# A sixth pair of up chunks by seven products in each MLP of a two-layer trunk, with down chunks cut in halves and read in another order

## The chip, the cores and the metric

The kernel runs on one core of a Trainium2 chip. The metric is the device time of one execution in microseconds, as the median of several. TensorE (PE) multiplies matrices into PSUM, its weight loads (PEld) overlap its matmuls; VectorE (DVE) and ScalarE (ACT) do elementwise work; GpSimd (POOL) does little here but issue transfers of its own queue; SyncE (SP) issues all others.

## The reference, cut to what matters

Two layers, each a token mixer and an MLP, all adding into one residual stream of 256 tokens by 2048 columns in float32. The change touches the two MLPs alone:

```python
D_MODEL = 2048; SEQ = 256; DEPTH = 2; D_FF = 4 * D_MODEL

def sq_relu_mlp(h, w_up, w_down):
    a = jax.nn.relu(h @ w_up)
    return (a * a) @ w_down

def reference(...):
    for i in range(DEPTH):
        ...
        h = rms_norm(x, mlp_norm_g[i])
        x = x + sq_relu_mlp(h, mlp_w_up[i], mlp_w_down[i]).astype(x.dtype)
    return x
```

## The kernel before, in words

**Split products.** Every float32 product is made of three: an operand is split into a rounded high part and the rest, and high by high, high by low and low by high are added up in PSUM (L447 to L449 for ordinary products, L1140 to L1142 for the wide ones). The tokens are the stationary side, in two tiles of 128; the weights stream through in tiles of 512 columns.

**Weight stream.** `plan` lists the loads of 256 rows by 512 columns (512 KB, five buffers `raw`), `units` the tiles that are split from them, both in the order in which TensorE will use them. `split` (L398, L399) casts a tile on ScalarE (`wh`) and subtracts on VectorE (`wl`), into five buffers each; it is called once for each unit used, so the splits run up to five units ahead. An ordinary unit is two blocks of 128 rows of one chunk of 512 columns: 2 x 2 token tiles x 3 = 12 matmuls.

**The MLP.** The 8192 inner columns are done in four quarters `b`. Each quarter has four up chunks `n` of 512 columns, each 16 row blocks `k` or 8 units, which give the turned activations `aT[n]`, and then four down chunks, again 16 row blocks each: `k // 4` says which `aT` is read. Up and down of the first quarter are counted from unit 0.

**Wide pairs.** For the pairs in `WIDE` two up chunks are computed together from quarters of the blocks, as a two-by-two product by seven products instead of eight. For each pair of row blocks `pr` there are three tiles (`crossed`, `differences`, `sums`) with two products of three matmuls each, and for each two of them one more tile: 28 tiles of 6 matmuls in all. VectorE makes the difference tile (L395) and the two halves of the sum tile (L401, L402) besides the three splits. `token_sums` makes the same sums of the tokens once per MLP. `WIDE_AT` is written by hand: it says after which ordinary unit each group of wide tiles stands. `wide_chain` then combines six PSUM banks (L1104 to L1111), and `turn_up` squares, transposes (L1058), writes to DRAM by POOL (L1052), loads back by SP (L354) and splits the turned activations (L1083 to L1090). The `free` keys hold the last step back until the previous quarter's `aT` has been read.

**Banks.** While wide work is woven in, six of the eight PSUM banks are its own, and all ordinary products share the two of one tag (`turn["only"]`), one for each token tile. The next product can start in a bank only when ScalarE has emptied it. The down products of the first three quarters are added by `add_chain` with `late`: ScalarE scales them into four small `y` tiles (L995), and POOL issues an accumulating transfer of each into `x` (L996). The last quarter has no wide work beside it at its end: three of its chunks run as a group, in the row parts of `LAST_DOWN_PARTS`, in three pairs of banks, and VectorE adds them (L999). `last_product` does the last chunk.

**Order.** `Jobs` runs the chains as generators: `tick` advances them after each row block or wide tile, so a chain's instructions stand in the engines' queues at the place where it was resumed; `pin` fixes that order on every engine.

Of the kernel before, what the change touches and what calls it, by code (L numbers as in the profile page):

```python
# [12 lines left out]
AF = mybir.ActivationFunctionType  # L13
# [4 lines left out]
P = 128  # L18
D = 2048
S = 256  # L20
# [21 lines left out]
LAST_DOWN_PARTS = ((0, 8), (8, 12), (12, 16))  # L42
# [6 lines left out]
WIDE = ((1, 0), (2, 0), (2, 2), (3, 0), (3, 2))  # L49
WIDE_AT = ((15, 19, 23, 27, 31, 34, 37, 39, 41, 42, 42, 43), (45, 47, 50, 53, 55, 58, 61, 63, 66, 67, 67, 68),  # L50
           (71, 74, 77, 79, 82, 85, 87, 90, 93, 93, 94, 95), (98, 101, 103, 106, 109, 111, 114, 117, 119, 119, 120, 120),
           (122, 125, 127, 130, 133, 135, 138, 141, 143, 143, 144, 145))
UP_ALONE = ((2, 3), (2, 3), (), ())


def wide_slots():

    for (b, n), at in zip(WIDE, WIDE_AT):
# [4 lines left out]
        for pr in range(0, KC // 2, 2):  # L63
            yield at[KC // 2 + pr // 2], (b, n, 3, pr)

# [54 lines left out]
def trunk(ctx: ExitStack, tc, x, fox_w_in, fox_b_f, fox_q_gain, fox_k_gain, fox_w_out, dil_w_in,  # L120
# [56 lines left out]
    wake(*[NC] * 8, S)  # L177
# [103 lines left out]
    def add(w, rows, cols):  # L281

        for r in range(rows[0], rows[1], RAW_SUB * P):
            units.append((len(plan), "rows"))
# [22 lines left out]
    def add_group(*chunks, parts=PARTS):  # L307

        for a, b in parts:
            for w, cols in chunks:  # L310
                add(w, (a * P, b * P), cols)
# [11 lines left out]
    def add_mlp(l):  # L323
# [3 lines left out]
        for b in range(4):  # L327
# [6 lines left out]
            add_group(*((down, [(n * NC, NC)]) for n in range(together)), parts=LAST_DOWN_PARTS)  # L334
            for n in range(together, NX):
                add(down, (0, D), [(n * NC, NC)])
# [100 lines left out]
    def product_steps(acc, keys, lhs, steps, post=None):  # L437

        for k in steps:
            jobs.need(keys(k))  # L440
            i = k % W_SUB
            hi, lo = (in_turn(w[:, i, :]) for w in splits[used[0]])
            ah, al = lhs(k)
            for t in range(NT):
                tok = slice(t * P, (t + 1) * P)
                first, last = k == 0, k == KC - 1
                nc.tensor.matmul(acc[t], ah[:, tok], hi, start=first, stop=False)  # L447
                nc.tensor.matmul(acc[t], ah[:, tok], lo, start=False, stop=False)  # L448
                nc.tensor.matmul(acc[t], al[:, tok], hi, start=False, stop=last)  # L449
            if post is not None and k == KC - 1:  # L450
                jobs.spawn(post(acc))
            if i == W_SUB - 1:
                used[0] += 1
# [868 lines left out]
```

## Time and profile before

| | |
|---|---|
| median of 3 runs | 2083.45 us (2082.98 to 2085.27) |
| span of the profiled execution | 2081.4 us |
| TensorE busy, matmuls | 2076.2 us, 9838 |
| VectorE busy | 1714.8 us |
| ScalarE busy | 1306.1 us |
| GpSimd busy | 275.1 us |
| moved by DMA | 539.04 MB, mean 259 GB/s |

The span is what lies between the first and the last instruction of the profiled execution; the timed runs also hold what lies around it. Busy time is the union of an engine's instructions. Matmuls overlap one another, so their durations don't add up to their time: the step from start to start does that. An engine that works through a queue in order can be idle because it is ahead; whether that matters is read from who waits for it.

### The profile page before, as it was taken

How to read it: one execution, taken by the hardware profiler on the slowest of the kernel's cores; microseconds unless marked ns; L12 is line 12 of the kernel's file. 1: busy time of each engine (PE TensorE's matmuls, PEld its weight loads, DVE VectorE, ACT ScalarE, POOL GpSimd, SP SyncE). 2: the span in 40 equal slices, each digit the busy share in tenths (PEclk: the TensorE clock that was granted, in tenths of full speed). 3: DMA queues.
4: the chain of work that ended last, by engine and by line, in shares of the span. 5: the costliest groups of instructions: out<-in, count | busy, mean ns of one | idle time of the engine just before them, and what ended most of it. 6: DMA issues, size and time to landing. Idle time of an engine off the chain costs nothing.

```text
span 2081.4 us, 28973 instructions
## 1 busy us (share of the span) xinstructions
PE 2076.2 (100%) x9838; PEld 1819.9 (87%) x9838; DVE 1714.8 (82%) x2183; ACT 1306.1 (63%) x1825; POOL 275.1 (13%) x398
## 2 busy tenths in 40 slices
PE   9999999999999999999999999999999999999999
PEld 7888888888888888888888888888888888888888
DVE  6888876898989889888668787766998898899874
ACT  6665654866666667664656565556766676666662
POOL 2000000111212112120010010000113031212120
PEclk9999999999999999999999999999999999999999
DMA  8888887888988898897877876867888888898885
GB/s 258 257 259 261 262 249 213 268 284 265 270 282 265 263 299 272 264 286 246 281 242 230 250 238 211 262 212 236 269 275 264 279 274 266 276 288 277 263 277 168
DMA packets 357205, 539.04 MB, mean 259 GB/s; under 512 B 43752, under 2 KB 144448, under 8 KB 357056
## 3 DMA queue, kind: packets, MB, share of 16 engines
q1 hardware_dynamic: 334624, 507.41, 76.6%
q0 software_dynamic: 22016, 29.38, 6.2%
q8 instruction: 77, 1.26, 0.2%
q10 hardware_dynamic: 416, 0.39, 0.1%
q14 instruction: 72, 0.59, 0.1%
HBM read 484.09 MB, written 40.39 MB: 252 GB/s over the span
## 4 chain that ended last, share of the span: by engine, by line
PE 98%; DVE 1%; ACT 1%; DMA 1%; issue 0%; SPq 0%; ACTq 0%
PE acc L447 26%; PE acc L448 26%; PE acc L449 26%; PE wide_n_tp L1140 2%; PE wide_n_tp L1141 2%; PE wide_n_tp L1142 2%; PE wide_n_sc L1141 2%; PE wide_n_acc L1140 2%; PE wide_n_sc L1140 2%; PE wide_n_acc L1142 2%; PE wide_n_sc L1142 2%; PE wide_n_acc L1141 2%; PE sc_d L800 0%; DVE wl L399 0%; DMA turned_n<-blocks_n 0%; PE sc_f L800 0%
## 5 line engine op out<-in xcount | busy, mean ns | idle before, releaser
L399 DVE TENSOR_TENSOR wl<-raw,wh 128x1024 fp32r<-128x1024 f32 (+1 forms) x763 | 919.9, 1215 | 302.4 <-ACT wh L398 295.2
L398 ACT CAST wh<-raw 128x1024 fp32r<-128x1024 f32 (+1 forms) x763 | 787.3, 1046 | 498.9 <-PE acc L449 370.1
L447 PE MATMUL acc<-wh,hT_n 128*128 128x512 f32 x1280 | 486.3, 380 | 0.0
L448 PE MATMUL acc<-wl,hT_n 128*128 128x512 f32 x1280 | 485.3, 379 | 0.2 <-DVE wl L399 0.2
L449 PE MATMUL acc<-wh,hT_n 128*128 128x512 f32 x1280 | 485.2, 379 | 0.0
L449 PEld LDWEIGHTS acc<-wh,hT_n 128*128 128x128 f32 x1280 | 241.9, 189 | 34.4 <-DVE hT_n L631 0.2
L448 PEld LDWEIGHTS acc<-wl,hT_n 128*128 128x128 f32 x1280 | 242.1, 189 | 33.7 <-DVE wl L399 0.9
L447 PEld LDWEIGHTS acc<-wh,hT_n 128*128 128x128 f32 x1280 | 242.1, 189 | 33.0 <-ACT hT_n L630 0.2
L447 PE MATMUL acc<-wh,aTh_n1a 128*128 128x512 f32 x512 | 194.0, 379 | 0.0
L448 PE MATMUL acc<-wl,aTh_n1a 128*128 128x512 f32 x512 | 194.0, 379 | 0.0
L449 PE MATMUL acc<-wh,aTl_n1a 128*128 128x512 f32 x512 | 194.0, 379 | 0.0
L447 PE MATMUL acc<-wh,aTh_n3a 128*128 128x512 f32 x480 | 181.9, 379 | 0.0
L448 PE MATMUL acc<-wl,aTh_n3a 128*128 128x512 f32 x480 | 181.9, 379 | 0.0
L449 PE MATMUL acc<-wh,aTl_n3a 128*128 128x512 f32 x480 | 181.9, 379 | 0.0
L996 POOL DMA_DIRECT2D x<-y_n x96 | 84.7, 1325 | 480.0 <-ACT y_n L995 421.1
L398 ACT CAST wh<-sd 128x1024 fp32r<-128x1024 f32 x80 | 84.1, 1051 | 101.9 <-DVE sd L395 78.5
L398 ACT CAST wh<-v 128x1024 fp32r<-128x1024 f32 x80 | 84.1, 1052 | 53.8 <-PE acc L449 41.4
L448 PEld LDWEIGHTS acc<-wl,aTh_n1a 128*128 128x128 f32 x512 | 96.8, 189 | 13.8
L449 PEld LDWEIGHTS acc<-wh,aTl_n1a 128*128 128x128 f32 x512 | 96.8, 189 | 13.7
L447 PEld LDWEIGHTS acc<-wh,aTh_n1a 128*128 128x128 f32 x512 | 96.8, 189 | 13.7
L399 DVE TENSOR_TENSOR wl<-v,wh 128x1024 fp32r<-128x1024 f32 x80 | 97.5, 1218 | 5.8 <-ACT wh L398 4.5
L395 DVE TENSOR_TENSOR sd<-raw,raw 128x1024 f32<-128x1024 f32 x80 | 97.4, 1218 | 5.5 <-DMA raw<-in_mlp_w_up_dram 5.5
(665 smaller groups left out, 3216.8 us busy)
## 6 DMA issues: line engine op xcount, KB each, us to landing
raw<-in_mlp_w_up_dram SPq DMA_DIRECT2D x296, 512.0 KB, 4.9
raw<-in_mlp_w_down_dram SPq DMA_DIRECT2D x256, 512.0 KB, 5.1
raw<-in_dil_w_in_dram SPq DMA_DIRECT2D x192, 256.0 KB, 3.5
raw<-in_fox_w_in_dram SPq DMA_DIRECT2D x94, 512.0 KB, 5.0
raw<-in_fox_w_out_dram SPq DMA_DIRECT2D x32, 512.0 KB, 4.9
raw<-in_dil_w_in_dram SPq DMA_DIRECT2D x32, 512.0 KB, 5.4
raw<-in_dil_w_out_dram SPq DMA_DIRECT2D x32, 512.0 KB, 4.5
x<-y_n POOLq DMA_DIRECT2D x96, 128.0 KB, 6.2
```

Of the source, the lines that this page charges most:

```text
L395: nc.vector.tensor_sub(quarters[0], raw, raws[n - 1][:, 1, :].unsqueeze(1).to_broadcast([P, RAW_SUB, NC]))
L398: nc.scalar.copy(hi[:, part, :], raw[:, part, :])
L399: nc.vector.tensor_sub(lo[:, part, :], raw[:, part, :], hi[:, part, :].bitcast(F32))
L447: nc.tensor.matmul(acc[t], ah[:, tok], hi, start=first, stop=False)
L448: nc.tensor.matmul(acc[t], ah[:, tok], lo, start=False, stop=False)
L449: nc.tensor.matmul(acc[t], al[:, tok], hi, start=False, stop=last)
L996: nc.gpsimd.dma_start(xt[n][:, t, h * HC:h * HC + HC], y, accum_op=ALU.add)
L1140: nc.tensor.matmul(banks[bank], ah, wh, start=what < 3 and of == 0, stop=False, **alone)
L1141: nc.tensor.matmul(banks[bank], ah, wl, start=False, stop=False, **alone)
L1142: nc.tensor.matmul(banks[bank], al, wh, start=False, stop=of == KC // 2 - 1, **alone)
```

## The change

It does five things, in both MLPs:

- `WIDE` takes in the pair (1, 2), so chunks 2 and 3 of quarter 1 leave `UP_ALONE`; `WIDE_AT` is written anew for six pairs over the fewer ordinary units, 160 instead of 176 per MLP.
- `HALVED`: in quarters 2 and 3, the first three down chunks are done in two halves of their rows. The first halves come first, each as a product of its own that is added late; the second halves follow, in quarter 3 as the group, whose parts now begin at row block 8.
- `place`: from quarter 1 on, the rows of down are read in the order of `aT[1]`, `aT[0]`, `aT[3]`, `aT[2]`, and the chains of a wide pair wait for `free` and `room` in that order.
- In products that share the one pair of banks, the first and the last unit run both row blocks for one token tile and then for the other, and the chains that empty the banks take the first tile while the second is still being multiplied (`ended`).
- The activations of a wide pair are spread: Relu at once, Square a step later (`turn`), and the evacuated tile's Relu isn't repeated.

The one wake matmul of 256 columns at the start becomes two of 128.

```diff
-LAST_DOWN_PARTS = ((0, 8), (8, 12), (12, 16))
+LAST_DOWN_PARTS = ((8, 12), (12, 16))
-WIDE = ((1, 0), (2, 0), (2, 2), (3, 0), (3, 2))
-WIDE_AT = ((15, 19, 23, 27, 31, 34, 37, 39, 41, 42, 42, 43), (45, 47, 50, 53, 55, 58, 61, 63, 66, 67, 67, 68),
-           (71, 74, 77, 79, 82, 85, 87, 90, 93, 93, 94, 95), (98, 101, 103, 106, 109, 111, 114, 117, 119, 119, 120, 120),
-           (122, 125, 127, 130, 133, 135, 138, 141, 143, 143, 144, 145))
-UP_ALONE = ((2, 3), (2, 3), (), ())
+WIDE = ((1, 0), (1, 2), (2, 0), (2, 2), (3, 0), (3, 2))
+WIDE_AT = ((15, 19, 23, 27, 30, 32, 33, 34, 37, 38, 39, 39),
+           (42, 44, 47, 49, 51, 52, 55, 56, 58, 58, 60, 61),
+           (64, 65, 67, 69, 71, 73, 75, 77, 79, 79, 79, 79),
+           (83, 85, 87, 88, 90, 91, 95, 97, 99, 99, 100, 101),
+           (102, 103, 104, 107, 108, 110, 112, 113, 115, 115, 116, 117),
+           (118, 120, 122, 123, 125, 126, 127, 128, 131, 131, 132, 132))
+UP_ALONE = ((2, 3), (), (), ())
+HALVED = (0, 0, 3, 3)
+HALF = KC // 2
+def place(b, k):
+    return k ^ 4 if b else k
...
-    wake(*[NC] * 8, S)
+    wake(*[NC] * 8, P, P)
...
+            for n in range(HALVED[b]):
+                add(down, (0, D // 2), [(n * NC, NC)], b)
...
+        def three(k, t):
...
+            first, last = k == begin, k == end
...
+        for k in steps[::W_SUB]:
+            rows = range(k, k + W_SUB)
+            by_block = post is not None and (k == begin or k + W_SUB > end)
+            ended = ("ended", used[0])
+            for i in range(W_SUB):
+                for r in rows if by_block and not i else () if by_block else rows[i:i + 1]:
+                    jobs.need(keys(r))
+                for r, t in [(r, i) for r in rows] if by_block else [(rows[i], t) for t in range(NT)]:
+                    three(r, t)
+                if by_block and k + W_SUB > end:
+                    if i:
+                        jobs.reach(ended)
+                    else:
+                        jobs.spawn(post(acc, ended))
...
+        for n in range(halved):
+            product(keys(0), lhs, lambda acc, ended, n=n: add_chain(acc, n, None, None, scale, True, ended), range(HALF))
         if group:
+            if halved:
+                jobs.done.add((scale, "halves"))
+                turn.update(next=1 - turn["only"], only=None)
...
         for n in range(group, NX):
+            begin = HALF if n < halved else 0
...
-        jobs.spawn(turn_up(squared(tiles[0], tiles[2]), key, n + 1, aT, (tag, "free", b - 1, n + 1), (key, "room", n)))
+        def turn(rows, at, *after):
+            for row in rows[at:]:
+                nc.scalar.activation(row, row, AF.Relu)
+            yield 1
+            yield from turn_up(rows, key, *after)
+
+        jobs.spawn(turn((tiles[0], tiles[2]), 0, n + 1, aT, (tag, "free", b - 1, n)))
         yield (key, "crossed", n)
...
-        yield from turn_up(squared(first, tiles[1]), key, n, aT, (tag, "free", b - 1, n))
+        yield from turn((first, tiles[1]), 1, n, aT, (tag, "free", b - 1, n + 1), (key, "room", n + 1))
```

## Rows read from the trace of the kernel before

**Rows 1.** The page: TensorE's totals, granted clock in 40 slices, chain by engine.

```profile
PE 2076.2 (100%) x9838; PEld 1819.9 (87%) x9838; DVE 1714.8 (82%) x2183; ACT 1306.1 (63%) x1825; POOL 275.1 (13%) x398
...
PEclk9999999999999999999999999999999999999999
...
PE 98%; DVE 1%; ACT 1%; DMA 1%; issue 0%; SPq 0%; ACTq 0%
```

**Rows 2.** Waits of TensorE over the span: us in total, times, longest us.

```profile
PE spare L175 <- DVE zeros L171: 1.1, 1, 1.1
PE acc L448 <- DVE wl L399: 0.2, 1, 0.2
```

**Rows 3.** Windows: us, busy (instructions) by engine, clock, DMA share, GB/s.

```profile
core 0: us, PE busy (x) PEld busy (x) DVE busy (x) ACT busy (x) POOL busy (x), PEclk, DMA share, GB/s
466.00:880.00 414.00, 414.00 (x1919) 362.24 (x1918) 370.40 (x380) 273.39 (x325) 83.32 (x128) 1.00 0.87 272
...
829.00:926.00 97.00, 97.00 (x451) 84.95 (x450) 86.38 (x89) 63.55 (x77) 19.57 (x30) 1.00 0.88 273
...
1800.00:1840.00 40.00, 40.00 (x187) 35.01 (x187) 34.41 (x35) 25.72 (x30) 11.73 (x17) 1.00 0.95 298
```

**Rows 4.** Timeline of VectorE at two wide groups: start us, us, instruction.

```profile
526.94 1.22 DVE L395 TENSOR_TENSOR sd<-raw,raw 128x1024 f32<-128x1024 f32 x1
528.07 1.22 DVE L399 TENSOR_TENSOR wl<-raw,wh 128x1024 fp32r<-128x1024 f32 x1
529.21 0.69 DVE L401 TENSOR_TENSOR v<-raw,sd 128x512 f32<-128x512 f32 x1
529.93 0.69 DVE L402 TENSOR_TENSOR v<-raw,v 128x512 f32<-128x512 f32 x1
530.54 1.22 DVE L399 TENSOR_TENSOR wl<-sd,wh 128x1024 fp32r<-128x1024 f32 x1
...
570.75 1.22 DVE L399 TENSOR_TENSOR wl<-sd,wh 128x1024 fp32r<-128x1024 f32 x1
```

**Rows 5.** Timeline of TensorE where those difference tiles are read.

```profile
531.46 0.38 PE L1140 MATMUL wide_n_sc<-wh,sums_n 128*128 128x512 f32 x1
531.81 0.48 PE L1141 MATMUL wide_n_sc<-wl,sums_n 128*128 128x512 f32 x1
...
575.95 0.38 PE L1141 MATMUL wide_n_sc<-wl,sums_n 128*128 128x512 f32 x1
```

**Rows 6.** Timeline of VectorE behind a wide pair's products; in brackets the idle time.

```profile
505.53 0.68 DVE L1104 TENSOR_TENSOR c_n1a<-c_n1a,wide_n_acc 128x512 f32<-128x512 f32 x1
...
506.97 0.69 DVE L1107 TENSOR_TENSOR c_n1a<-c_n1a,wide_n_sc 128x512 f32<-128x512 f32 x1
507.57 0.68 DVE L1108 TENSOR_TENSOR c_n1a<-c_n1a,wide_n_sc 128x512 f32<-128x512 f32 x1
...
513.47 2.36 DVE L399 TENSOR_TENSOR wl<-raw,wh 128x1024 fp32r<-128x1024 f32 x2 [1.75 <-ACT wh L398]
515.75 0.71 DVE L1058 STREAM_TRANSPOSE turned_n1a<-c_n1a 128x512 f32<-128x512 f32 x1
516.37 1.19 DVE L395 TENSOR_TENSOR sd<-raw,raw 128x1024 f32<-128x1024 f32 x1
```

**Rows 7.** Timeline of ScalarE: activations of that pair, a cast, an evacuation.

```profile
510.02 2.47 ACT L1117 ACTIVATE c_n1a<-c_n1a 128x512 f32<-128x512 f32 x4 [1.92 <-DVE c_n1a L1110]
...
528.24 1.04 ACT L398 CAST wh<-sd 128x1024 fp32r<-128x1024 f32 x1 [2.90 <-DVE sd L395]
...
531.69 1.56 ACT L995 ACTIVATE y_n<-acc,rstd_n 128x256 f32<-128x256 f32 x4
```

**Rows 8.** The page's transfers: KB each, median us from issue to landing.

```profile
x<-y_n POOLq DMA_DIRECT2D x96, 128.0 KB, 6.2
```

**Rows 9.** Durations in ns, min/median/max, of lines L399 and L996.

```profile
L399 DVE TENSOR_TENSOR wl<-raw,wh x763: 681/1221/1248, 5.6 to 2065.6; 128x1024 fp32r<-128x1024 f32 x189, 128x512 fp32r<-128x512 f32 x2
...
L996 POOL DMA_DIRECT2D x<-y_n x96: 837/1226/1914, 496.8 to 1991.1; - x96
```

**Rows 10.** Waits of ScalarE, 381 to 1017 us: us in total, times, longest us.

```profile
ACT wh L398 <- DMA raw<-in_mlp_w_up_dram: 12.4, 10, 3.5
```

More of the change, by code (lines that the diff above doesn't have):

```diff
@@ L435, in sums, with product_steps @@
         return [pool.tile([P, NC], F32, tag=tag, name=f"acc{used[0]}_{t}") for t in range(NT)]
[L437 to L442, printed above, removed]
-            ah, al = lhs(k)
[L444 to L453, printed above, removed]
-                if "opening" not in issued:
-                    split()
-            jobs.tick()
-            if i == W_SUB - 1 and woven["do"]:
+    def product_steps(acc, keys, lhs, steps, post=None, begin=0, end=KC - 1):
+        def three(k, t):
+            hi, lo = (in_turn(w[:, k % W_SUB, :]) for w in splits[used[0]])
+            ah, al = lhs(k)
+            tok = slice(t * P, (t + 1) * P)
+            first, last = k == begin, k == end
+            nc.tensor.matmul(acc[t], ah[:, tok], hi, start=first, stop=False)
+            nc.tensor.matmul(acc[t], ah[:, tok], lo, start=False, stop=False)
+            nc.tensor.matmul(acc[t], al[:, tok], hi, start=False, stop=last)
+        for k in steps[::W_SUB]:
[12 more added lines that the diff above has]
+                        jobs.spawn(post(acc, ended))
+                if i == W_SUB - 1:
+                    used[0] += 1
+                    if "opening" not in issued:
+                        split()
+                jobs.tick()
+            if woven["do"]:
@@ L983, in dilated, with add_chain @@
                 product(keys_h(tag), lhs_h(tag), value_post)
-    def add_chain(acc, n, then, ready, scale, late):
+    def add_chain(acc, n, then, ready, scale, late, ended=None):
         yield scale and (scale, "rstd") or 0
         for t in range(NT):
+            if t and ended:
+                yield ended
             at = halves(xt[n][:, t, :])
@@ L1034, in up_chain, with turn_up @@
         for t in range(NT):
+            if t and ended:
+                yield ended
             nc.scalar.activation(halves(rows[t]), by_column(acc[t]), AF.Relu)
         yield clear(1)
-        def squared(t):
+        yield from turn_up(rows, key, n, aT)
+    def turn_up(rows, key, n, aT, free=None, behind=None):
+        for t in range(NT):
             nc.scalar.activation(rows[t], rows[t], AF.Square)
-            return rows[t]
-        yield from turn_up(squared, key, n, aT)
-    def turn_up(squared, key, n, aT, free=None, behind=None):
-        rows = [squared(t) for t in range(NT)]
         yield 2
```

62 lines of the change are left out of this document (27 added, 35 removed).

## The prediction

> **What bounds the kernel now.** I read the totals of the page and its chain first: TensorE is busy for 100% of the span, the chain that ended last is 98% matmuls, and the granted clock stands at its full 2.4 GHz level in all 40 slices [rows 1]. Busy time of overlapping matmuls does not prove that the engine streams without holes, so the waits of TensorE come next: two, 1.1 us ahead of the first data and 0.2 us later [rows 2]. Last comes the rate: 1919 matmuls touch a stretch of 414.00 us [rows 3], so one starts every 414 / 1918 = 0.216 us. The kernel is a stream of matmuls at that step, and the time falls only with their number, as long as everything else arrives in time.
>
> What arrives is the split weight tile, cast by ScalarE (L398) and completed by VectorE (L399). VectorE is the second bound: in the stretch that holds one wide pair, 829 to 926 us, it is busy 86.38 of 97.00 us [rows 3]. How far ahead it runs is read by setting the end of a tile's L399 against the matmul that reads it. A calm example: the tile of the differences ends at 570.75 + 1.22 = 571.97 us and is read at 575.95, a lead of 4.0 us. A tight one: ended at 531.76, read at 531.81, and TensorE stepped 0.35 us instead of 0.216 there [rows 4, 5]. So the old spacing of the pairs already touches the edge at one place of each MLP.
>
> **What is removed.** A pair of up chunks computed alone is 2 chunks x 16 row blocks x 2 token tiles x 3 = 192 matmuls of 512 columns; by seven products it is 28 tiles x 6 = 168. Two MLPs save 2 x 24 = 48 matmuls, at 0.216 us: 10.4 us. The down chunks keep their number of matmuls; halving them only changes where an accumulation starts. The duration of a single matmul, 0.38 us [rows 5], would make it 18.2 us, but durations overlap, so the step is the price. The Trainium skill, "TensorE: Matmul & The Clock Gate", section "Back-to-back issue gap", gives about 131 ns for one 512-column matmul in a sustained stream of weight loads and matmuls; by that page the saving would be 6.3 us. This trace disagrees: its sustained step is 216 ns [rows 3].
>
> **What is added on VectorE.** In order, from start to next start in rows 4: a split 1.14 us, the difference tile (L395) 1.13, the two sums (L401, L402) 0.72 and 0.61. The six combinations of a pair (L1104 to L1111) take 1.44 for the first two and about 0.60 for each of the others, 3.8 us in all, and a transpose 0.62 [rows 6]. For the closing subtractions of the turned tiles I take 0.60 as for combinations of their size. A wide pair thus costs 28 x 1.14 + 8 x 2.46 + 3.8 + 4 x 0.62 + 4 x 0.60 = 60.3 us of VectorE against 168 x 0.216 = 36.3 us of TensorE; an ordinary unit (two row blocks of one chunk) costs 1.14 against 12 x 0.216 = 2.59 us. The check on before: its last pair lies over 24 units, 27.4 + 60.3 = 87.7 of 62.2 + 36.3 = 98.5 us, 89%; the row says 86.38 of 97.00, 89% [rows 3].
>
> The new slots put the six pairs over 27, 22, 19, 19, 16 and 15 units, where five had 30, 26, 27, 24 and 24. VectorE against TensorE becomes 91 of 106 us, 85 of 93, 82 of 85.5, 82 of 85.5, 78.5 of 77.7, and 77.4 of 75.1. So the last two pairs of each MLP ask for 3.1 us more than there is, and inside a pair the demand is uneven: three tiles of a slot group need 5.9 us of VectorE in 3.9 us of TensorE. The dense runs are units 30 to 34 (5 x 1.14 + 4 x 5.88 = 29.2, with some 4 for the transposes and token sums of the start 33, in 5 x 2.59 + 4 x 3.88 = 28.5), 102 to 108 (7 units and 5 groups: 37.4, with two transposes and four subtractions of the pair before 41.0, in 37.5) and 118 to 128 (11 and 8: 59.6, with the same 63.2, in 59.5). Each falls short by 3.5 to 4.5 us, and the lead that it can use up is about 3 to 4 us. The lead is capped by five buffers: in ordinary units 4 x 2.59 less a cast and a split, 8 us; in wide ones half of that.
>
> One hole goes with each pair: ScalarE waits for the combinations, then runs four activations (2.47 us) before the next cast, and VectorE sat idle for 1.75 us behind it [rows 6, 7]. The change takes two of the four activations to a later step, which shortens the hole by some 1.2 us, and saves one repeated Relu, 2.47 / 4 = 0.62 us. ScalarE itself keeps room: 63.55 of 97.00 us [rows 3], and a pair more in each MLP adds 12 casts of 1.04 us [rows 7] and the evacuations below.
>
> **Evacuations and their queue.** Six half products more per MLP bring 24 activations on ScalarE (four take 1.56 us [rows 7]) and 24 accumulating transfers on the queue of POOL, 1.23 us of issue each and 6.2 us to land [rows 8, 9]. POOL has room: 19.57 of 97.00 us busy [rows 3]. Behind a waiting transfer stand the writes of turned tiles, and behind a busy y buffer ScalarE itself and so the casts. The tightest place is the three halves at units 128 to 139, 10.4 us apart without slots between: a buffer is free after about 0.4 + 2 x 1.23 + 6.2 = 9.1 us for the first token tile and up to 0.8 + 4 x 1.23 + 6.2 = 11.9 for the second. A wait of 1 to 2 us of ScalarE there is covered by the lead of ordinary units, 8 us; without it, it would be 1 to 2 us per MLP.
>
> Where a product ends without a slot behind it (units 63 and 135), the next one wants the same two banks. The new order by token tile leaves 6 x 0.216 = 1.3 us to empty a bank; two activations need 0.8 us plus what ScalarE is in the midst of, at most one cast of 1.04. Cost: 0 to 0.6 us at each, taken as 0.3, four times, 1.2 us. Turning the row order (aT[1] before aT[0]) is free: the matmuls are the same, and chunk 3 of the last quarter is read 11 units and four tiles after its products end (33.7 us), where before 11 units (28.5 us) sufficed. The last 27 units of each MLP hold no wide work, so the norm and the final product keep their cover. The wake at the start is the same 256 columns in two pieces, ahead of the first data: nothing.
>
> **DMA.** Over units 102 to 132 the loads are 71 x 0.524 MB, the accumulations 28 x 0.131, turned tiles about 4.2: 45 MB in 153 us, 295 GB/s. Before, the stretch 829 to 926 moved 273 GB/s at a busy share of 0.88; the fullest one I found is 298 at 0.95 [rows 3]. It fits, barely; ScalarE already waited for raw up tiles ten times in the first MLP, up to 3.5 us [rows 10], and with less lead such a wait reaches TensorE. I bound it by 0 and 3 us per MLP.
>
> **The sum.** Saving 10.4. Stalls: in each MLP three dense runs of 0 to 2 us, taken as 0.6, nearer to the 0.13 us of the one place that fell short than to the whole gap; banks 0.6; late tiles 0 to 3, taken as 0.3, as their waits of before cost TensorE nothing that shows: 2.7 us, and twice that 5.4; the 0.3 us that before loses at 531 us and at the same place of the second MLP is small change beside it. Net -5.0 us. The span 2081.4 becomes 2076.4; around it lie 2.05 us up to the median of 2083.45, so 2078.4. No stall at all gives 2073.1.
>
> **The rivals.** First, nearly all is given back: VectorE and the raw tiles together cost 3 to 7 us per MLP (dense runs at their full shortfall of 3.5 to 4.5 us, with a lead as small as at 531 us). Time 2079.3 to 2087.6. For it: the lead of 0.05 us at 531 us under a lighter load; against it: before, TensorE's waits name L399 with 0.2 us only [rows 2], and the hole behind the combinations gets shorter. Second, no stall: 2073.1 to 2075, if the lead at the entry of each run is above 4 us, as in the calm example. Third, slower: VectorE becomes the bound over the last three pairs (units 83 to 132). It decides where its step from start to start rises to the full duration, 1.22 instead of 1.14 us for a split and 0.69 instead of 0.60 for half a tile [rows 4]: a pair costs 64.5 us, so 87.7 of 85.5, 84.0 of 77.7 and 82.8 of 75.1, 16 us short, less 4 of lead: 12 us per MLP, 24 in all, 2097. Anything over 7.3 us per MLP ends on this side. Against it: the check on before holds at the shorter step. Fourth, that POOL stops VectorE: 24 issues of 1.23 us in the dense part would take 29.5 us per MLP from it; with the 3 us shortfall, less a lead of 4 us, that is 57 us in all on top of 2073.1, so 2130. The trace speaks against it: no split of the full size ran longer than 1.248 us against a median of 1.221, while the accumulate issues range from 0.837 to 1.914 us [rows 9]; if one waits, it is POOL. The Trainium skill, "GPSIMD Engine Reference", section "1. Specifications", has this as a rule: GpSimd shares its SBUF interfaces with VectorE and contends with VectorE instructions of two SBUF inputs, which the splits are.
>
> **How the numbers follow.** Forecast (part given back, 2075 to 2079.3) 0.45; no stall 0.15; nearly all given back 0.27; VectorE or DMA as the bound, over 2087.6, 0.11; POOL stopping VectorE 0.02. A measurement of this kernel can tell about 0.2%, 4.2 us, from no change, so faster is the first two, 0.60; same 0.27; slower 0.13. The range leaves out only the lowest edge and the slow cases: 2072.8 to 2087.0.
>
> **What would show it.** 9838 matmuls less 48 (one wake more). TensorE's waits, and its steps of over 0.216 us in the timeline: each that L399 releases is a dense run that fell short; I expect them near units 30 to 34, 102 to 108 and 118 to 128, 0.3 to 2 us each. VectorE busy at 95% or more over the last two pairs, with idle time before L399 nearly gone. If its idle time stays at 10% while TensorE waits, the shortage is raw tiles or ScalarE, not VectorE. If the waits name an evacuated bank, the bank step was mis-sized. The forecast is wrong if the waits sum to over 6 us, or to none.

## The result and the profile after

The changed kernel takes 2092.98 us (median of five runs, 2091.39 to 2093.61) against 2083.48 us for the kernel before on the same chip: a ratio of 1.0041, 95% interval 1.0028 to 1.0053. It is slower by 9.5 us, where the prediction had 2078.4 us, faster by 5, and a range up to 2087.0.

The page of the changed kernel (busy time, share of the span, instructions; then the granted clock in 40 slices and the chain that ended last), as [rows 1]:

```profile
span 2091.9 us, 29264 instructions
PE 2074.1 (99%) x9791; PEld 1809.8 (87%) x9791; DVE 1782.8 (85%) x2267; ACT 1336.6 (64%) x1889; POOL 319.8 (15%) x446
...
PEclk9999999999999999999999999999999999999999
...
PE 76%; DVE 11%; DMA 6%; issue 4%; ACT 2%; POOL 0%; SPq 0%; DVEq 0%; ACTq 0%
```

The saving is there: 9791 matmuls, 48 fewer than before and one wake more. But the chain is no longer 98% matmuls: 11% of it runs over VectorE, 6% over transfers. The waits of TensorE (us in total, times, longest us) name two releasers that [rows 2] do not have at this size:

```profile
PE acc L457 <- ACT y_n L1020: 6.9, 7, 1.9
PE wide_n_sc L1168 <- DVE wl L412: 4.6, 9, 0.9
...
PE acc L458 <- DVE wl L412: 0.7, 3, 0.3
```

L457 <- L1020 is a product that waits for ScalarE to empty its bank; L1168 and L458 wait for VectorE's part of a split, L412. The view doesn't count the steps that are only a little long. For the full price I went through the timeline of TensorE from 381 us on (ahead of it there are no wide products), took every step from one 512-column matmul to the next, and put what it has over 0.216 us to its releaser (after each wait one step of 0.32 us follows, which goes to the same one). One profiled execution of each kernel gives:

| | before | after |
|---|---|---|
| waits for VectorE's splits (L412) | 0.92 us | 9.59 us |
| waits for banks (ScalarE's L1020) | 0 | 9.57 us |
| steps of 0.427 us behind the longest bank wait | 0 | 1.68 us |
| all, with small ones | 0.92 us | 20.95 us |

48 matmuls at 0.216 us save 10.4; 20.95 - 0.92 = 20.0 is given back; 9.6 us net, and the spans differ by 2091.9 - 2081.4 = 10.5. So this table holds all but 0.9 us of the result.

**VectorE.** The stretches of the first MLP that hold the dense runs (busy us of each engine, granted clock, share and rate of DMA), to be set against the windows in [rows 3]:

```profile
766.00:840.00 74.00, 72.43 (x333) 62.08 (x331) 73.26 (x79) 52.30 (x69) 22.89 (x32) 1.00 0.95 281
840.00:910.00 70.00, 69.23 (x320) 60.00 (x319) 68.24 (x74) 47.96 (x61) 15.95 (x24) 1.00 0.89 284
```

VectorE (the third number) is busy 73.26 of 74.00 us and 68.24 of 70.00, where [rows 3] had 86.38 of 97.00. One of its stalls, first VectorE, then TensorE:

```profile
901.62 0.69 DVE L414 TENSOR_TENSOR v<-raw,sd 128x512 f32<-128x512 f32 x1
902.34 0.69 DVE L415 TENSOR_TENSOR v<-raw,v 128x512 f32<-128x512 f32 x1
902.95 1.22 DVE L412 TENSOR_TENSOR wl<-sd,wh 128x1024 fp32r<-128x1024 f32 x1
904.08 1.22 DVE L412 TENSOR_TENSOR wl<-raw,wh 128x1024 fp32r<-128x1024 f32 x1
```

```profile
903.36 0.38 PE L1167 MATMUL wide_n_sc<-wh,sums_n 128*128 128x512 f32 x1
904.22 0.48 PE L1168 MATMUL wide_n_sc<-wl,sums_n 128*128 128x512 f32 x1 [0.49 <-DVE wl L412]
```

VectorE runs without a gap, ends the split at 902.95 + 1.22 = 904.17, and TensorE goes on at 904.22. Its lead is zero, where the calm example of [rows 4, 5] had 4.0 us.

The lead is not gone for good between the dense runs. Here are a split just ahead of the run of units 102 to 108, one from the middle of the stretch between the runs, and one just ahead of the run 118 to 128; below them are the matmuls that read these tiles (of the two merged splits of a row the second is meant):

```profile
773.02 2.35 DVE L412 TENSOR_TENSOR wl<-raw,wh 128x1024 fp32r<-128x1024 f32 x2
847.24 1.23 DVE L412 TENSOR_TENSOR wl<-raw,wh 128x1024 fp32r<-128x1024 f32 x1 [0.20 <-ACT wh L411]
853.36 2.35 DVE L412 TENSOR_TENSOR wl<-raw,wh 128x1024 fp32r<-128x1024 f32 x2
```

```profile
778.65 0.38 PE L458 MATMUL acc<-wl,aTh_n1a 128*128 128x512 f32 x1
853.81 0.38 PE L1168 MATMUL wide_n_tp<-wl,hT_n 128*128 128x512 f32 x1
858.99 0.38 PE L458 MATMUL acc<-wl,aTh_n1a 128*128 128x512 f32 x1
```

The leads are 778.65 - 775.37 = 3.3 us, 853.81 - 848.47 = 5.3 us and 858.99 - 855.71 = 3.3 us. VectorE, which had no lead left at 815.6 us, is ahead again at 847 us, where it even waits for a cast, and loses the lead once more by 904 us. In the second MLP the same three tiles have leads of 3.3, 5.3 and 3.3 us.

**Banks.** The longest such wait of the first MLP is the product end at unit 63 (ScalarE first; the bracket is the idle time ahead of an instruction and what ended it):

```profile
601.07 1.05 ACT L411 CAST wh<-raw 128x1024 fp32r<-128x1024 f32 x1 [2.95 <-DMA raw<-in_mlp_w_up_dram]
602.03 0.61 ACT L1113 CAST aTh_n1a<-back_n1a 128x512 fp32r<-128x512 f32 x1
602.55 0.59 ACT L1153 ACTIVATE c_n1a<-wide_n_tp 128x512 f32<-128x512 f32 x1
603.04 1.04 ACT L411 CAST wh<-sd 128x1024 fp32r<-128x1024 f32 x1
603.98 0.62 ACT L1146 ACTIVATE c_n1a<-c_n1a 128x512 f32<-128x512 f32 x1
604.50 1.14 ACT L1076 ACTIVATE c_n1a<-c_n1a 128x512 f32<-128x512 f32 x2
605.54 1.03 ACT L411 CAST wh<-raw 128x1024 fp32r<-128x1024 f32 x1
606.48 0.47 ACT L1020 ACTIVATE y_n<-acc,rstd_n 128x256 f32<-128x256 f32 x1
```

```profile
605.20 0.38 PE L459 MATMUL acc<-wh,aTl_n1a 128*128 128x512 f32 x1
607.36 0.48 PE L457 MATMUL acc<-wh,aTh_n1a 128*128 128x512 f32 x1 [1.78 <-ACT y_n L1020]
```

The first token tile's last matmul starts six steps ahead of 605.20, at 603.9, so its bank could be emptied from 604.3 on. ScalarE had stood still 2.95 us for a raw tile, and then ran what stood ahead of the evacuation in its queue, 5.4 us of casts and activations, to 606.48. The tile was asked for late: SP issued it at 595.21 us, as soon as VectorE's split of 593.96 us had ended and freed a buffer, and ScalarE had it 5.9 us later. The loads as a whole did not become slower: the median from issue to landing of the up loads is 4.9 us, as before. Over the whole span SP's queue stands longer than before for the buffers that the sum L414 frees; for the same sum (then L401) it had stood 192.4 us:

```profile
SPq L386 <- DVE v L414: 269.4, 94, 5.4
SPq L367 <- DMA held_n3a<-turned_n3a: 39.6, 24, 4.2
```

And ScalarE's waits for raw up tiles, of which [rows 10] show some, sum to 71.7 us now; over the same view before it is 26.1 us. This sum is no measure of the bank waits, as e1 and e9 will show; what counts is whether such a wait stands just ahead of an evacuation:

```profile
ACT wh L411 <- DVE sd L408: 110.7, 77, 3.8
ACT wh L411 <- DMA raw<-in_mlp_w_up_dram: 71.7, 52, 3.3
```

The longest bank wait of the second MLP adds SP. SP first (the first row merges two issues, and SP stands still between them), then ScalarE, then TensorE:

```profile
1876.18 4.99 SPq L367 DMA_DIRECT2D back_n3a<-held_n3a  x2
1881.27 0.38 SPq L386 DMA_DIRECT2D raw<-in_mlp_w_down_dram  x1
```

```profile
1886.45 1.05 ACT L411 CAST wh<-raw 128x1024 fp32r<-128x1024 f32 x1 [2.08 <-DMA raw<-in_mlp_w_down_dram]
1887.41 1.04 ACT L411 CAST wh<-v 128x1024 fp32r<-128x1024 f32 x1
1888.35 1.56 ACT L1020 ACTIVATE y_n<-acc,rstd_n 128x256 f32<-128x256 f32 x4
```

```profile
1886.96 0.38 PE L1169 MATMUL wide_n_sc<-wh,sums_n 128*128 128x512 f32 x1
1889.24 0.48 PE L457 MATMUL acc<-wh,aTh_n3a 128*128 128x512 f32 x1 [1.90 <-ACT y_n L1020]
...
1890.77 0.63 PE L459 MATMUL acc<-wh,aTl_n3a 128*128 128x512 f32 x1
1891.20 0.63 PE L457 MATMUL acc<-wh,aTh_n3a 128*128 128x512 f32 x1
```

SP stands at two loads of turned activations, because their writes have not landed; the raw load behind them goes out at 1881.27, is there 5.2 us later, and two casts further the bank is emptied. Behind that wait seven steps of 0.43 us follow. Two of the shorter bank waits (868 and 1948 us, 0.9 us together) have another start: the cast ahead of the evacuation waits for a difference tile of VectorE.

### The profile page after: what moved, and what is told of

It reads as the page before. It is cut to its first block, busy times and chain, and to the rows that moved or that the text cites. A ratio compares the mean times of both kernels' runs of the same rounds, so it can differ in the third digit from the quotient of the medians.

```text
span 2091.9 us, 29264 instructions
## 1 busy us (share of the span) xinstructions
PE 2074.1 (99%) x9791; PEld 1809.8 (87%) x9791; DVE 1782.8 (85%) x2267; ACT 1336.6 (64%) x1889; POOL 319.8 (15%) x446
## 4 chain that ended last, share of the span: by engine, by line
PE 76%; DVE 11%; DMA 6%; issue 4%; ACT 2%; POOL 0%; SPq 0%; DVEq 0%; ACTq 0%
PE acc L457 20%; PE acc L458 20%; PE acc L459 20%; DVE wl L412 7%; DMA raw<-in_mlp_w_up_dram 3%; DMA raw<-in_mlp_w_down_dram 2%; DVE sd L408 2%; PE wide_n_tp L1169 2%; PE wide_n_tp L1168 2%; PE wide_n_tp L1167 2%; PE wide_n_sc L1168 1%; PE wide_n_sc L1169 1%; PE wide_n_sc L1167 1%; PE wide_n_acc L1169 1%; PE wide_n_acc L1168 1%
## 5 line engine op out<-in xcount | busy, mean ns | idle before, releaser
L412 DVE TENSOR_TENSOR wl<-raw,wh 128x1024 fp32r<-128x1024 f32 (+1 forms) x755 | 910.7, 1213 | 240.9 <-ACT wh L411 232.2
L457 PE MATMUL acc<-wh,hT_n 128*128 128x512 f32 x1152 | 437.9, 380 | 0.2 <-ACT hT_n L653 0.2
L458 PE MATMUL acc<-wl,hT_n 128*128 128x512 f32 x1152 | 437.0, 379 | 0.5 <-DVE wl L412 0.5
L459 PE MATMUL acc<-wh,hT_n 128*128 128x512 f32 x1152 | 436.8, 379 | 0.0
L459 PEld LDWEIGHTS acc<-wh,hT_n 128*128 128x128 f32 x1152 | 217.7, 189 | 31.4 <-DVE hT_n L654 0.4
L458 PEld LDWEIGHTS acc<-wl,hT_n 128*128 128x128 f32 x1152 | 217.9, 189 | 30.8 <-DVE wl L412 1.8
L457 PEld LDWEIGHTS acc<-wh,hT_n 128*128 128x128 f32 x1152 | 217.9, 189 | 30.1 <-ACT hT_n L653 0.4
L1021 POOL DMA_DIRECT2D x<-y_n x144 | 128.8, 1242 | 524.2 <-ACT y_n L1020 522.5
L457 PE MATMUL acc<-wh,aTh_n1a 128*128 128x512 f32 x512 | 194.6, 380 | 3.7 <-ACT y_n L1020 3.7
L458 PE MATMUL acc<-wl,aTh_n1a 128*128 128x512 f32 x512 | 194.2, 379 | 0.1
L457 PE MATMUL acc<-wh,aTh_n3a 128*128 128x512 f32 x480 | 183.1, 382 | 3.3 <-ACT y_n L1020 3.2
L458 PE MATMUL acc<-wl,aTh_n3a 128*128 128x512 f32 x480 | 182.9, 381 | 0.2 <-DVE wl L412 0.2
L411 ACT CAST wh<-sd 128x1024 fp32r<-128x1024 f32 x96 | 100.7, 1049 | 116.8 <-DVE sd L408 110.7
L408 DVE TENSOR_TENSOR sd<-raw,raw 128x1024 f32<-128x1024 f32 x96 | 116.9, 1218 | 8.5 <-DMA raw<-in_mlp_w_up_dram 7.4
L411 ACT CAST wh<-v 128x1024 fp32r<-128x1024 f32 x96 | 100.9, 1051 | 36.2 <-PE acc L459 17.9
L412 DVE TENSOR_TENSOR wl<-v,wh 128x1024 fp32r<-128x1024 f32 x96 | 116.7, 1216 | 3.5 <-ACT wh L411 3.2
L412 DVE TENSOR_TENSOR wl<-sd,wh 128x1024 fp32r<-128x1024 f32 x96 | 116.6, 1215 | 0.5 <-ACT wh L411 0.4
L457 PEld LDWEIGHTS acc<-wh,aTh_n1a 128*128 128x128 f32 x512 | 96.8, 189 | 19.3 <-ACT y_n L1020 5.7
L458 PEld LDWEIGHTS acc<-wl,aTh_n1a 128*128 128x128 f32 x512 | 96.8, 189 | 14.2 <-DVE wl L412 0.6
```

The source lines that it names most:

```text
L408: nc.vector.tensor_sub(quarters[0], raw, raws[n - 1][:, 1, :].unsqueeze(1).to_broadcast([P, RAW_SUB, NC]))
L411: nc.scalar.copy(hi[:, part, :], raw[:, part, :])
L412: nc.vector.tensor_sub(lo[:, part, :], raw[:, part, :], hi[:, part, :].bitcast(F32))
L1021: nc.gpsimd.dma_start(xt[n][:, t, h * HC:h * HC + HC], y, accum_op=ALU.add)
```

## The experiments

Theory: two shortages. VectorE has nothing to spare in the dense runs from unit 83 on and is late by itself; and evacuations stand in ScalarE's queue behind casts whose raw tile is late, because buffers come free late or because SP stands still at a back load. The rivals: one shortage only (all waits are VectorE's); the missing slots alone; the accumulating transfers. "Excess" below is the sum of steps over 0.216 us as in the table above, from the one profiled execution of each kernel; the ratio is against runs of the kernel before on the same chip. For each version with six pairs whose excess the table gives, the median of before, less 10.4 us for the 48 steps, plus the excess over the 0.92 us of before, comes within 0.9 us of the time of that profiled execution. So the steps account for the time.

| | median us | ratio, 95% interval | excess us | VectorE | banks |
|---|---|---|---|---|---|
| changed kernel | 2092.98 | 1.0041, 1.0028 to 1.0053 | 20.95 | 9.59 | 9.57 |
| e1 no sums | 2079.9 | 0.9982, 0.9973 to 0.9992 | 9.25 | 0.45 | 8.71 |
| e2 slots moved | 2096.01 | 1.0060, 1.0042 to 1.0079 | 21.68 | 8.35 | 3.93 |
| e3 five pairs | 2087.4 | 1.0018, 1.0008 to 1.0027 | 6.00 | 1.05 | 4.96 |
| e4 no accumulations | 2087.87 | 1.0019, 1.0010 to 1.0029 | 17.52 | 10.22 | 6.99 |
| e5 back loads later | 2091.25 | 1.0036, 1.0023 to 1.0048 | 18.35 | 10.74 | 6.45 |
| e6 sums on POOL | 2214.24 | 1.0623, 1.0607 to 1.0639 | | | |
| e9 back later, slot | 2088.4 | 1.0020, 1.0010 to 1.0029 | 14.77 | 9.28 | 4.38 |
| e10 three causes | 2075.82 | 0.9961, 0.9946 to 0.9975 | 2.81 | 0 | 1.63 |
| e11 four halves | 2104.18 | 1.0101, 1.0084 to 1.0118 | 29.70 | 10.81 | 3.85 |
| e12 even slots | 2129.51 | 1.0216, 1.0199 to 1.0233 | 57.63 | 14.87 | 8.08 |

**e1, VectorE's part taken away.** The sums are left out and the sum tile is split from the difference tile; loads and matmuls stay.

```diff
-            nc.vector.tensor_add(quarters[1][:, 0, :], raw[:, 0, :], quarters[0][:, 1, :])
-            nc.vector.tensor_sub(quarters[1][:, 1, :], raws[n - 1][:, 0, :], quarters[1][:, 0, :])
+            pass
```

> The changed kernel without the two VectorE instructions that make the sum tile (L414, L415); the split of the sums reads the difference tile instead, so the sums are wrong numbers. That takes 1.33 us of VectorE from each of 96 slot groups, 64 us in each MLP, and frees the raw tiles earlier. Theory V (VectorE has no time left in the dense runs, and its lateness spreads to casts, evacuations and loads): TensorE's steps of over 0.216 us nearly all go, evacuated banks included, 2073 to 2076 us. Theory B (the banks are late by themselves, at product ends without a slot behind them): the waits that name L1020 stay at some 9 us, 2081 to 2085. Theory T (the 48 more accumulating transfers hold up the loads): raw tiles stay late, 2086 or more.

The waits of TensorE in this kernel:

```profile
PE acc L456 <- ACT y_n L1019: 6.1, 5, 1.7
...
PE acc L457 <- DVE wl L412: 0.2, 1, 0.2
```

VectorE's waits are gone (9.59 to 0.45 us), the banks' stay (9.57 to 8.71, the half-speed steps aside). So they are two shortages, and the rival of one alone falls. The banks' stay in sum, not place by place: the ends of unit 63 still cost 1.55 and 1.60 us, the wait at 944 us falls from 1.48 to 0.13, and the one at unit 108 of the first MLP grows from 0.17 to 1.84, where SP again stands at a back load. ScalarE's waits for raw up tiles halve meanwhile, from 71.7 to 36.8 us. The edit also takes VectorE below its load of before, so it says that these waits are VectorE's, not what a sixth pair adds to them.

**e2, the missing slots.** The third pair begins after unit 63 instead of 64, and the last tile of the sixth moves to unit 135, so that both product ends have wide work behind them.

```diff
-           (64, 65, 67, 69, 71, 73, 75, 77, 79, 79, 79, 79),
+           (63, 65, 67, 69, 71, 73, 75, 77, 79, 79, 79, 79),
-           (118, 120, 122, 123, 125, 126, 127, 128, 131, 131, 132, 132))
+           (118, 120, 122, 123, 125, 126, 127, 128, 131, 131, 132, 135))
```

> The changed kernel with one wide slot moved behind each of the two product ends that have none (64 to 63, and the last 132 to 135). Theory B: the four waits at those places (1.94, 1.48, 0.98 and 0.64 us, with 0.10 after each) go, 5.4 us, and the time is 2087 to 2088. Theory V: ScalarE is late there because VectorE and the raw tiles are late, and a slot covers 1.3 to 3.9 us of it but the shortage comes out elsewhere: 1 to 4 us less, 2089 to 2092. Theory T: within 1 us of 2093.

The bank waits at 605, 944, 1683 and 2024 us go, 5.6 us of banks in all. The tile at 135 makes the turned activations late: 7.7 us of waits for `aTl` (L1117, L1120) appear, with 1.7 us of half-speed steps behind one, and the time doesn't fall. The slot at 63 is free to take, the one at 135 is not. The missing slots alone are thus not the cause: with both filled, 8.35 us of VectorE's waits and 3.93 us at other banks are left.

**e3, five pairs.** Everything of the change but the sixth pair: pairs, slots and lone chunks of before (chunk 3 now ahead of 2), with halves, row order, token tile order and spread activations.

```diff
-WIDE = ((1, 0), (1, 2), (2, 0), (2, 2), (3, 0), (3, 2))
+WIDE = ((1, 0), (2, 0), (2, 2), (3, 0), (3, 2))
-UP_ALONE = ((2, 3), (), (), ())
+UP_ALONE = ((2, 3), (3, 2), (), ())
```

(`WIDE_AT` as before.)

> All of the change but the sixth pair: the five pairs and their slots of before, chunks 3 and 2 of quarter 1 alone, with the halves, the row order, the order by token tile and the spread activations kept. Matmuls as before. Theory V: no shortage, 2083 to 2085. Theory B: two product ends per MLP without a slot (units 147 and 151) cost 1 to 2 us each, 2087 to 2090. Theory T: the 48 more accumulating transfers alone bring late raw tiles, 2086 to 2090.

The preparations alone cost 6.00 - 0.92 = 5.1 us of TensorE, nearly all at the ends of half products of the last quarter (0.70 us at 931.6, 1.52 at 942.8, 2.17 at 2018.5). VectorE's waits are 1.05 us here, so all but a little of the 9.59 us comes with the sixth pair and its slots. ScalarE and POOL at 943:

```profile
943.11 0.62 ACT L1110 CAST aTh_n1a<-back_n1a 128x512 fp32r<-128x512 f32 x1 [1.45 <-DMA back_n1a<-held_n1a]
943.63 1.56 ACT L1017 ACTIVATE y_n<-acc,rstd_n 128x256 f32<-128x256 f32 x4
```

```profile
936.40 2.91 POOL L1079 DMA_DIRECT2D held_n1a<-turned_n1a  x3
941.87 0.55 POOL L1079 DMA_DIRECT2D held_n1a<-turned_n1a  x1 [2.56 <-DMA x<-y_n]
```

Writes of turned activations stand on POOL's queue until accumulating transfers of the halves land, the loads back come late, ScalarE waits in a cast for them, and the evacuation stands behind that cast.

**e4, the accumulating transfers.** The 48 of the first halves are left out, the evacuations stay.

```diff
-                    nc.gpsimd.dma_start(xt[n][:, t, h * HC:h * HC + HC], y, accum_op=ALU.add)
+                    if not drop:
+                        nc.gpsimd.dma_start(xt[n][:, t, h * HC:h * HC + HC], y, accum_op=ALU.add)
```

> The changed kernel with the first halves' 48 accumulating transfers left out (ScalarE still writes the y tiles; the halves never reach x, so the output lacks them). Theory T: the loads land earlier and most of the 20 us of waits go, 2080 to 2085. Theory V: 0 to 3 us less than 2093, as POOL and the transfers are not what is short. Theory B: 2092 to 2094.

Excess falls by 3.4 us, all of it at banks (the wait at 1887 and its half-speed steps go, 944 falls from 1.48 to 0.85, 2024 from 0.64 to 0.14). VectorE's waits don't fall (10.22). The profiled execution was the slowest of the ten runs; the medians, each set against before on its chip, fall by 5.3 us. So the accumulating transfers are worth 3 to 5 of the 20 us: a part of the bank waits, and not the cause of the whole.

**e5, SP's stops.** The back loads are issued three steps later.

```diff
-            yield 1
+            yield 4
             back.append(work.tile([P, NC], F32, tag="w", name=f"back_{key}_{n}_{t}", bufs=6))
```

> The changed kernel with the loads of the turned tiles (L1100, on SP) placed three steps later in SP's queue, when their writes have landed. Theory Q (late evacuations come from late raw tiles, and these from SP standing still in front of such a load, 3.6 us at 1876 and 4.2 us at 1881): the two waits behind that (2.06 us and 1.6 us of half clock at 1887, 0.17 to 0.66 us at 809 to 830) go, those of L412 stay at some 9 us, 2086 to 2090. Theory L (raw tiles are late because five buffers do not cover 5 to 6 us to landing at the pace of the dense runs, whatever SP does): 2091 to 2094.

Banks fall from 9.57 to 6.45 us and the half-speed steps go, VectorE rises by 1.2 and waits for `aTl` of 1.0 us appear: 2.6 us of excess in all. The medians differ by less than their intervals, so alone this is indicated, not shown.

**e6, e7, e8, the sums on POOL.** The two sums of each group move to POOL, alone, then with the later back loads (e7), then with the slot at 63 too (e8).

```diff
-            nc.vector.tensor_add(quarters[1][:, 0, :], raw[:, 0, :], quarters[0][:, 1, :])
-            nc.vector.tensor_sub(quarters[1][:, 1, :], raws[n - 1][:, 0, :], quarters[1][:, 0, :])
+            nc.gpsimd.tensor_add(quarters[1][:, 0, :], raw[:, 0, :], quarters[0][:, 1, :])
+            nc.gpsimd.tensor_sub(quarters[1][:, 1, :], raws[n - 1][:, 0, :], quarters[1][:, 0, :])
```

> The changed kernel with the two sums (L414, L415) on POOL instead of VectorE: the same result. Theory V: VectorE has 64 us per MLP more, the 9.6 us of L412 waits go as in the run without the sums, the late evacuations stay, 2080 to 2084. Against it, theory P (POOL and VectorE block each other on their two-input work, or POOL's writes and accumulations queue behind the sums): L412 grows beyond 1.25 us or the turned tiles come late, 2090 to 2105.

> Both edits together. Theories V and Q: both kinds of waits go but for the two product ends without a slot behind them, 2075 to 2080. Theories V and L: as with the sums on POOL alone, within 1.5 us. Theory P: no better than the later loads alone.

> Both edits, and the first slot of the third pair at unit 63, behind a product end that had none. Theory B (at 605 and 1683 us the bank is late since no wide tile stands behind the product's end): 2.0 and 1.1 us less than the run before this, 2072 to 2077. Theory L: ScalarE is as late there as before, and the slot hides 2.6 us of it, so the same gain in part, or none if the next cast is late instead.

2214.24, 2217.19 (1.0640, 1.0624 to 1.0655) and 2212.06 us (1.0615, 1.0599 to 1.0631): 130 us slower, with or without the other edits. The lines of e6 (duration in ns: lowest, median, highest):

```profile
L412 DVE TENSOR_TENSOR wl<-sd,wh x96: 1175/2166/3076, 404.4 to 2117.9; 128x1024 fp32r<-128x1024 f32 x96
L414 POOL TENSOR_TENSOR v<-raw,sd x96: 1281/2140/5926, 403.5 to 2116.8; 128x512 f32<-128x512 f32 x96
```

In the changed kernel the same split of `sd` reads 1181/1218/1226. A sum takes 2.14 us on POOL instead of 0.68 on VectorE, and the split that runs beside it is stretched from 1.22 to 2.17 us. VectorE can't be relieved in this way.

**e9, two of the causes.** Back loads later, and the slot at 63.

```diff
-           (64, 65, 67, 69, 71, 73, 75, 77, 79, 79, 79, 79),
+           (63, 65, 67, 69, 71, 73, 75, 77, 79, 79, 79, 79),
-            yield 1
+            yield 4
```

> The changed kernel with back loads four steps later (L1094) and the first slot of the third pair after unit 63 instead of 64. Theory (SP stands still ahead of back loads, and the product end at unit 63 has no slot): the two add up. The first was worth 1.7 us of median, the second takes the waits at 605 and 1683 us, 2.9 us. So 2087 to 2089, TensorE's excess 15 to 16 us, of it VectorE 10, banks 3.5, no half-clock stretch. Rival (all of it is one shortage of VectorE, and what is taken from one wait appears in the next): 2091 as before it, the excess moves to L412.

2088.4 us and 14.77 us of excess: the two add up, and the interval (1.0010 to 1.0029) only just touches that of the changed kernel. VectorE's waits stay (9.28), and so do ScalarE's waits for raw up tiles (71.6 us), while the bank waits are halved. Of the versions with six pairs that compute everything this is the fastest, and still slower than the kernel before.

**e10, all three.** As e9, and the sums left out as in e1.

> All three named causes are taken away at once: the sums L414 and L415 are left out (the sum tiles are split from the difference tile, so the output isn't the reference's), back loads come four steps later, and the third pair starts after unit 63. If the list of causes is complete: TensorE's excess falls from 20.95 to 3 to 5 us (the product end at unit 135 stays), and the time is 2073 to 2077, the saving of 10.4 us less that. If another cause stands behind them: excess 8 us or more and 2079 or above, as with the sums alone left out.

```profile
PE acc L456 <- ACT y_n L1019: 0.9, 1, 0.9
```

The bank wait left (1.1 us at 2005) is that of unit 135, the product end that still has no slot behind it. VectorE's waits are gone. e1 took 11.7 us of excess away and e9 6.2; together 17.9, and e10 has 18.1. The time follows: 2084.02 on this chip less 10.4 plus 2.81 - 0.92 makes 2075.5, and 2075.82 was measured. So the list of causes is complete to within 2 us, and the saving of 10.4 us is real.

**e11, four halves.** As e9, with the fourth down chunk of the last quarter in halves too, and the slots of the sixth pair over units 118 to 135.

```diff
-HALVED = (0, 0, 3, 3)
+HALVED = (0, 0, 3, 4)
-           (118, 120, 122, 123, 125, 126, 127, 128, 131, 131, 132, 132))
+           (118, 121, 123, 125, 127, 128, 129, 131, 133, 134, 135, 135))
```

> As the first of these three, with all four down chunks of the last quarter in halves, so that the turned activations of the last pair are read four units (10.4 us) later, and its slots over units 118 to 135 instead of 118 to 132. Eight accumulating transfers per MLP less two are added. Theory (VectorE's shortage of the last pair is its spacing): the waits on L412 at 903 to 936 and 1983 to 1998 us go, 2.5 to 3.5 us, the product end at unit 135 has a slot now (about 2 us more): excess 10 to 12 us, 2083 to 2086. Rival (the last three pairs share one shortage, and accumulations cost ScalarE what the spacing gives): 2086 to 2089, with new waits for y buffers on ScalarE.

A miss: 2104.18 us. VectorE's waits in the run 118 to 128, whose slots were spread, do go in both MLPs (2.4 and 2.2 us in e9, none here); those of the run 102 to 108, whose slots are as in e9, stay (2.1 and 2.2 us). But 4.0 us of others appear in units 6 to 16 of the second MLP, and 12.2 us of new ones stand at the start of the next layer (waits for the turned tokens `hT` and slow steps behind them, 1003 to 1028 us, the longest 3.0 us). The last product is half as long now and, it seems, no longer covers the norm that follows:

```profile
PE acc L457 <- ACT hT_n L590: 4.2, 2, 2.8
...
PE acc L459 <- DVE hT_n L591: 3.5, 2, 2.9
```

**e12, even slots.** As e9, and the last three pairs with slots two units apart.

```diff
-           (83, 85, 87, 88, 90, 91, 95, 97, 99, 99, 100, 101),
-           (102, 103, 104, 107, 108, 110, 112, 113, 115, 115, 116, 117),
-           (118, 120, 122, 123, 125, 126, 127, 128, 131, 131, 132, 132))
+           (81, 83, 85, 87, 89, 91, 93, 95, 97, 98, 98, 99),
+           (100, 102, 104, 106, 108, 110, 112, 114, 115, 115, 116, 116),
+           (117, 119, 121, 123, 125, 127, 128, 130, 131, 131, 132, 132))
```

> The changed kernel with back loads four steps later and the third pair from unit 63, as in the pair of edits run before, and in addition the slots of the last three pairs two units apart each (81 to 99, 100 to 116, 117 to 132) instead of in dense runs. If unevenness inside the pairs makes VectorE late (the prediction's dense runs): the waits on L412 fall from 9.3 to 3 to 5 us and the time from 2088.4 to 2082 to 2085. If the shortage is of the sum over units 81 to 132 (VectorE asks for as much as there is): L412 stays at 8 to 10 us, in other places, and the time at 2087 to 2090.

A miss for both theories: 2129.51 us. Two waits of 10.0 and 7.6 us for turned activations that ScalarE casts too late, and waits for the wide banks of the pair before (L1132, L1153) take the lead. VectorE's waits rise to 14.87 us, of which 3.8 lie in units 6 to 16 of the second MLP, where no slot was moved. ScalarE at the longer one:

```profile
965.77 0.47 ACT L1020 ACTIVATE y_n<-acc,rstd_n 128x256 f32<-128x256 f32 x1 [5.26 <-DMA x<-y_n]
...
971.30 2.18 ACT L1113 CAST aTh_n1a<-back_n1a 128x512 fp32r<-128x512 f32 x4
```

ScalarE stands 5.26 us for a `y` buffer. Whether unevenness or the sum makes VectorE late was not told apart by this: the slots are tied to the chains of the pairs, and moving them moved those. The leads in the trace of the changed kernel, and e11, do tell it.

## Why the prediction was wrong, step by step

The prediction gave 5.4 us of the saving back, the trace 20.0. The 14.6 us between them are 10.0 at the banks (9.57 + 1.68, taken as 1.2), 5.1 at VectorE (9.59 - 0.92, taken as 3.6), less 0.6 that stood for late tiles and is in the banks; small steps make up the 0.1 left.

**The saving** held: 48 matmuls at 0.216 us, and with the causes removed (e10) the time comes out at that sum. **The price of VectorE's work** held as well: a split still starts 1.13 us after the one ahead of it (902.95 and 904.08), and VectorE is as full as was worked out (99% and 97% of the two windows).

**The step that failed first is the bank step**: 0.3 us at each of two ends per MLP were taken, 0.6 the bound. The two places were right, the ends of units 63 and 135, the sizes 1.94 and 1.48 us in the first MLP (605 and 944 us), 0.98 and 0.64 in the second. Ends with slots behind them came on top, the one at 1887 with its half-speed steps above all. What failed is "two activations need 0.8 us plus what ScalarE is in the midst of, at most one cast": the evacuation doesn't follow the instruction in progress but all that stands ahead of it in the queue, of which a cast may wait for its tile (2.95 us at 601). The prediction had named its own sign for this, waits that name an evacuated bank, and the trace shows it.

**The second is the size of the dense runs**, taken as 0.6 us each from the one place of before that fell short [rows 4, 5], with 2 as the bound. By units, the run 102 to 108 cost 1.8 us in the first MLP and 1.7 in the second (770 to 840, 1850 to 1920 us), the run 118 to 128 with unit 133 behind it 2.1 and 2.4, the run 30 to 34 nothing; the rest, 1.5 us, is a place ahead of the wide work (381 to 385 us, where before lost 0.45) and one at 1815.

The lead was not what failed. The prediction gave each run 3 to 4 us of its own, and the trace has 3.3 us at units 102 and 118 of both MLPs, with 5.3 us in between. That is so although by the prediction's figures the pairs over units 83 to 132 ask for 82 + 78.5 + 77.4 = 238 us of VectorE, and TensorE gives them 85.5 + 77.7 + 75.1 = 238. (The run 30 to 34, which lost nothing, was entered with 4.6 us.) What was too small is the shortfall inside a run, 3.5 to 4.5 us, which was added up over whole runs, and with it the 0.6 us that was taken as the rest after the lead. From the entry of the run 118 to 128 to the stall shown above VectorE works 904.17 - 855.71 = 48.5 us; TensorE takes 904.22 - 858.99 = 45.2 us, of which 1.2 are waits, so 44.0 of work. VectorE is 4.4 us short by unit 126, over a lead of 3.3. In the run 102 to 108 it is 4.3 us short as early as unit 104 (21.1 against 16.8 us), since three groups stand in its first three units. Once the lead is zero, each further unit with a group costs its whole gap: 0.53 us at unit 127 and again at 128, close to the 7.02 - 6.47 = 0.55 of the prediction's steps. These sums come from the one trace of the changed kernel; e11, where the wider slots take the waits of the one run away and leave those of the other, agrees with them.

**Late raw tiles** were bounded at 0 to 3 us per MLP and taken as 0.3, with the argument that such waits had cost TensorE nothing. That was so in the kernel before, where no wait for a bank shows. In the new kernel such a wait reaches TensorE where an evacuation stands close behind it (601, 942 and 1886 us); it can't be added to the bank term, for it is its cause. **POOL's queue** was named with the right victims (writes of turned tiles, then ScalarE), but priced at nothing: "covered by the lead of ordinary units", and else 1 to 2 us per MLP. The cover was not there, as ScalarE also had banks to empty: e3, with five pairs, shows 2.2 us in the first MLP and 2.3 in the second, and in the changed kernel e4 puts the accumulating transfers at 3 to 5 us in all. **SP's queue** was not looked at: a load of turned activations that waits for its write holds up the raw loads behind it, for up to 4.2 us at one such load, and at 1876 us two of them follow one another.

**The rivals.** "Nearly all is given back" had the right mechanism for one half, and its 3 to 7 us per MLP hold for VectorE (4.3); the banks, kept at 0.6 there too, make it 10 per MLP. The third rival, VectorE at its full duration from start to start, did not occur; its bound, slower from 7.3 us per MLP on, is what decided the sign, by another cause. The fourth was rightly rejected for transfers: with 48 issues more no split ran longer than 1.244 us. e6 shows that POOL's own sums do stretch VectorE's. The Trainium skill, "GPSIMD Engine Reference", section "1. Specifications", states the contention for VectorE's instructions with two SBUF inputs; e6 agrees (2.17 us for a split instead of 1.22), and this case shows it for POOL's arithmetic, not for its issues.

The range stopped at 2087.0 because it left the slow cases out, which had 0.13. The prediction's own bounds reach further: three runs of 2 us, two ends of 0.6 and 3 us of late tiles per MLP make 20.4 us in all, and 2093.5. The measured time lies just inside that, but not by the same terms: the banks with the late tiles behind them cost 11.3 us, where 8.4 was the bound, and VectorE 8.7, where it was 12.

## What to carry to other kernels

Where work comes in bursts, follow the second engine's lead through each burst and price it by the place where the lead is smallest, not by the sum over the whole burst: here the lead came back to 5.3 us between two bursts, and each still cost about 2 us. An evacuation on an engine that works in order costs what stands ahead of it in the queue, waits included: go through that queue, and through SP's and POOL's, instruction by instruction at each place where a bank or buffer has no slack. A change that saves work on the bound engine and asks for more from the second is worth what remains after both, and that can be tried by leaving the second engine's work out, as e10 does.

## What the runs showed of the hardware

A sum of 128 x 512 with two inputs takes 2.14 us on POOL (median), and VectorE's split beside it 2.17 instead of 1.22 us. Of the 96 splits of difference tiles in e6, the 80 that overlap a sum on POOL have that median, and the 16 that overlap none have 1.22 us. POOL's issues of transfers did nothing of the kind.

After the wait of 1.9 us at 1887 TensorE ran seven steps of 0.43 us, and the granted clock of that stretch is 0.51, the 1.2 GHz level:

```profile
1890.00:1893.50 3.50, 3.50 (x10) 2.78 (x9) 3.46 (x5) 2.61 (x3) 2.64 (x3) 0.51 0.98 259
```

The wait of 1.78 us at 605 had no such steps behind it. In e2 a wait of 2.01 us (to 2035.7) had them and one of 2.07 us (to 954.5) had not, so the length of the hole alone does not tell. A hole near 2 us can cost 1.7 us more than itself; what tells the cases apart, the runs here do not show.
